# f of the SwiGLU blocks turned by VectorE and DRAM instead of by TensorE, for 10 of 11 groups

## The chip, the cores and the metric

One core of one Trainium2 chip runs the whole program. The metric is the device time of one execution in microseconds (us), and less is better. Before the change the median of three runs is 1397.9 us (1396.51 to 1398.93).

## What is computed

The program is a chain of transformer blocks over 256 tokens of width 1024: SwiGLU, gMLP, SwiGLU, SwiGLU, latent attention, SwiGLU, then a block of retention and forgetting attention, and a last SwiGLU. The change touches the five SwiGLU blocks alone. What they compute, cut to what matters:

```
def swiglu(n, w_gate, w_up, w_down):            # n: 256 x 1024
    return (silu(n @ w_gate) * (n @ w_up)) @ w_down
# w_gate, w_up: 1024 x 2816     w_down: 2816 x 1024     all float32
```

The product silu(...) * (...) is called f in the kernel: 256 tokens by 2816 columns.

## The kernel before, in words

**Tiles.** The 256 tokens are two streams of 128, t = 0 and t = 1, each an object `st` with a Python generator (`stream`). Weights come from DRAM in chunks of 128 x 1024 float32 (512 KB). `fetch` (L153) loads a chunk into `raw` (RAW = 3 buffers) from SyncE's queue (L158), and `split` (L336) makes of it a pair: `hi`, the float32r cast, by ScalarE (L337), and `lo`, the rest `raw - hi`, by VectorE (L338). The pairs have RING = 9 buffers each. `mm3` (L166) multiplies two such pairs in three matmuls (L167, L168, L169).

**Steps.** The main loop (L1134) runs over steps s. Each step fetches chunk s + 2 (AHEAD = 2), then lets stream 0 use chunk s and stream 1 use chunk s - 5 (LAG = 5). A chunk is 6 matmuls of 512 columns for each stream, so a step is 12. `later(st, n, fn)` (L192) has `fn` issued after n further chunks of that stream.

**A SwiGLU block** (`ffn`, L357) has NG = 11 groups j of 256 columns of f. `up(j)` takes four chunks (tile `g`, 512 columns: 256 of gate, 256 of up), then makes `th` by a tanh on ScalarE (L364) and f by two operations on VectorE (L365, L367). f has the tokens on the partitions. `turn(j)` (L372), two chunks later, turns it: two 128 x 128 transposes on TensorE against the identity (L376) into the PSUM tile `tr`, and `split` from there into `fth` and `ftl`, which have f's columns on the partitions. `down(j)` (L383) multiplies them with two chunks of w_down and adds to the accumulators `a`. The order is up(0), up(1), down(0), up(2), down(1), and so on: a group of six steps for every j. So f of j = 0 is used five steps after the one that ends it, f of a later j seven steps after. In the last block down(8), down(9) and down(10) stand together at the end.

There are 5 blocks x 2 streams x 11 groups = 110 turns.

**Order.** The framework's scheduler orders each engine's instructions when the program is built, by priority (the order of the program, raised inside `urgent()`) among those whose inputs it takes to be there. Each queue then runs in that order, and an instruction that waits holds those behind it. SyncE's queue carries all the loads: the chunks, and now and then gains and constants (`prepare`, L261, L265 and L266, which wait for a one-column copy on GpSimd, `touch`, L196).

**Tags.** Tiles of one tag share buffers: `th` and `f` have two each, `fth` and `ftl` three (six in the last groups of the last block).

Of the kernel before, what the change touches and what calls it, by code (L numbers as in the profile page):

```python
# [9 lines left out]
F32 = mybir.dt.float32  # L10
F32R = mybir.dt.float32r
# [5 lines left out]
P = 128  # L17
D = 1024
KD = D // P
FF = 2816  # L20
NG = FF // 256
# [88 lines left out]
def body(ctx: ExitStack, tc: tile.TileContext, a: dict, out: bass.AP, stop=None, dbg=None):  # L110
    nc = tc.nc
    V, S, G, PE = nc.vector, nc.scalar, nc.gpsimd, nc.tensor

    base = ctx.enter_context(tc.tile_pool(name="base", bufs=1))
    ring = ctx.enter_context(tc.tile_pool(name="ring", bufs=1))
    psg = ctx.enter_context(tc.tile_pool(name="psg", bufs=2, space=bass.MemoryType.PSUM))
    psa = ctx.enter_context(tc.tile_pool(name="psa", bufs=1, space=bass.MemoryType.PSUM))
    pst = ctx.enter_context(tc.tile_pool(name="pst", bufs=2, space=bass.MemoryType.PSUM))

    def f32(x):  # L120
        return x.bitcast(F32)
# [70 lines left out]
    def later(st, n, fn, *args):  # L192

        st.later.append([n + 1, fn, args])
# [128 lines left out]
    def acc_tile(st):  # L323
        return [psa.tile([P, 512], F32, name=f"a{st.t}{q}") for q in range(2)]

    def g_tile():
        return psg.tile([P, 512], F32, name="g")
# [8 lines left out]
    def split(hi, lo, src):  # L336
        S.copy(hi, src)  # L337
        V.tensor_tensor(lo, src, f32(hi), op=ALU.subtract)  # L338

    def rows_gemm(acc, lhs, w, k, first, last):  # L340

        for q in range(2):
            mm3(acc[q], sl(lhs, slice(None), k), sl(w, slice(None), slice(512 * q, 512 * q + 512)), first, last)

    def unit(st, ps, lhs=None, nq=4, nk=2, n=512):

        for q in range(nq):
            w = yield
            k_gemm(ps, lhs or st.xt, w, nk * q, q == 0, q == nq - 1, nk, n)
# [7 lines left out]
    def ffn(st, inner={}, last=False):  # L357
        fts = {}

        def up(j):  # L360
            ps = g_tile()
            yield from unit(st, ps)
            th = base.tile([P, 256], F32, name="th", tag="th", bufs=2)
            S.activation(th, ps[:, :256], AF.Tanh, scale=st.ch)  # L364
            V.scalar_tensor_tensor(th, th, 1.0, ps[:, :256], op0=ALU.add, op1=ALU.mult)  # L365
            f = base.tile([P, 256], F32, name="f", tag="f", bufs=2)
            V.scalar_tensor_tensor(f, th, st.cc, ps[:, 256:], op0=ALU.mult, op1=ALU.mult)  # L367
            fts[j] = f
            st.mark = f[:, 0:1]
            later(st, 2, turn, j)  # L370

        def turn(j):  # L372
            f = fts[j]
            tr = pst.tile([P, 4, P], F32, name="tr")
            for k in range(2):
                PE.transpose(tr[:, k, :], f[:, k * P:(k + 1) * P], ident)  # L376
            pool, n = (enter("last"), 6) if last and j > 5 else (base, 3)
            hi = pool.tile([P, 2, P], F32R, name="fth", tag="fth", bufs=n)
            lo = pool.tile([P, 2, P], F32R, name="ftl", tag="ftl", bufs=n)
            split(hi, lo, tr[:, :2, :])  # L380
            fts[j] = hi, lo

        def down(j):  # L383
            if j == 0:
                st.acc = acc_tile(st)
            for k in range(2):
                w = yield
                f = fts[j]
                rows_gemm(st.acc, f, w, k, j + k == 0, j == NG - 1 and k == 1)

        for j in range(NG):
            yield from up(j)
            if 0 < j < NG - 2 * last:
                yield from down(j - 1)
            if callable(inner.get(j)):
                inner[j]()
            elif j in inner:
                yield from inner[j]
        for j in range(NG - 1 - 2 * last, NG):
            yield from down(j)  # L400
# [614 lines left out]
    def enter(name):  # L1015
        if name not in pools:
            pools[name] = [tc.alloc_tile_pool(name=name, bufs=1), 0]
        return pools[name][0]
# [92 lines left out]
    n = len(chunks)  # L1111
# [38 lines left out]
def layout(i):  # L1150

    c = np.ascontiguousarray
    o = {}

    def cols(w, unit, nk=2):

        k, n = w.shape
        return c(w.reshape(k // (P * nk), nk, P, n // unit, unit).transpose(3, 0, 2, 1, 4)).reshape(-1, P, nk * unit)

    def rowsw(w):  # L1160

        return w.reshape(-1, P, w.shape[1])

    def gu(g, u):
        both = np.stack([g.reshape(D, NG, 256), u.reshape(D, NG, 256)], 2).reshape(D, NG * 512)
        return cols(both, 512)

    fl = [(i["ffn_w_gate"][l, k], i["ffn_w_up"][l, k], i["ffn_w_down"][l, k]) for l in range(2) for k in range(2)]
    fl.append((i["w_gate_2"][0], i["w_up_2"][0], i["w_down_2"][0]))
    for n, (g, u, d) in enumerate(fl):  # L1170
        o[f"gu{n}"] = gu(g, u)
        o[f"dn{n}"] = rowsw(d)
    o["win"] = cols(i["gmlp_w_in"][0], 512)
    o["wgo"] = rowsw(i["gmlp_w_out"][0])
    o["wdq"] = cols(i["mla_w_dq"][0], 512)
    o["wdkv"] = cols(i["w_dkv"], 320)
    uq = i["mla_w_uq"][0].reshape(512, NH, 192)
    o["wuqr"] = cols(c(uq[:, :, P:]).reshape(512, 512), 512)
    o["wuq"] = cols(c(uq[:, [0, 2, 4, 6, 1, 3, 5, 7], :P]).reshape(512, 1024), 512)
    ukv = i["w_ukv"].reshape(256, NH, 256)  # L1180
    o["wukv"] = np.concatenate([cols(c(ukv[:, :, k * P:(k + 1) * P]).reshape(256, 1024), 512) for k in range(2)])
    wo = i["mla_w_o"][0].reshape(NH, P, D)
    o["wo"] = c(wo[[0, 2, 4, 6, 1, 3, 5, 7]])
    w2 = i["w_in_2"][0]
    big = np.concatenate([w2[:, 1536:2048], w2[:, 2048:2560], w2[:, 2560:3072], w2[:, 0:512], w2[:, 512:1024],
                          w2[:, 1024:1536], w2[:, 3080:4104], w2[:, 4104:5128]], 1)
    o["w2"] = cols(big, 512)
    o["w2f"] = c(w2[:, 3072:3080].reshape(8, P, 8).transpose(1, 0, 2)).reshape(P, 64)
    o["wro"] = rowsw(i["w_ret_o_2"][0])
    o["wfo"] = rowsw(i["w_fox_o_2"][0])  # L1190
    o["wout"] = rowsw(i["w_out_2"][0])
    gl = [i["ffn_pre_g"][0, 0], i["ffn_pre_g"][0, 1], i["ffn_pre_g"][1, 0], i["ffn_pre_g"][1, 1], i["mix_pre_g"][0],
          i["mix_pre_g"][1], i["kv_norm_g"], i["kv_a_norm_g"], i["mla_q_norm_g"][0], i["g_mix_2"][0], i["g_ffn_2"][0], i["g_ret_norm_2"][0],
          np.concatenate([i["g_fox_q_2"][0]] * 2), np.concatenate([i["g_fox_k_2"][0]] * 2)]
    o["pre"] = np.stack([gl[k] for k in (4, 1, 2, 5, 3, 9)])
    o["kva"], o["qn"] = i["kv_a_norm_g"].reshape(1, 256), i["mla_q_norm_g"].reshape(1, 512)
    o["gains"] = c(np.concatenate([g.reshape(-1, P).T for g in gl], 1))
    o["ffn_post_g"] = c(i["ffn_post_g"].reshape(4, D))
    o["mix_post_g"] = c(i["mix_post_g"])
    o["gmlp_ln_g"] = c(i["gmlp_ln_g"])  # L1200
    o["gmlp_ln_b"] = c(i["gmlp_ln_b"])
    o["b_forget_2"] = c(i["b_forget_2"])
    o["ws"] = c(i["gmlp_w_s"][0].transpose(2, 0, 1)).reshape(P, 16 * P)
    o["bs"] = c(i["gmlp_b_s"][0].T)
    o["x"] = c(i["x"][0])
    o["positions"] = c(i["positions"].reshape(2, P).T)
    o["c1"], o["c2"] = constants()
    return o
# [49 lines left out]
```

## Time and profile before

| | before |
|---|---|
| median of three runs | 1397.9 us |
| profiled execution, its own time | 1396.79 us |
| its span in the profile | 1394.9 us |
| TensorE busy | 1376.0 us |
| VectorE busy | 957.0 us |
| ScalarE busy | 717.2 us |
| TensorE clock granted, mean | 1.0 of full speed |
| share of the 16 DMA engines, chunk queue | 57.7% |

The span is 1.9 us shorter than the profiled execution's time; that much lies around it. Busy times of engines overlap, so they don't add up to the span. Matmuls are pipelined: a matmul's own duration in the profile is longer than the distance to the next one's start, and that distance is what the engine's time is made of.

### The profile page before, as it was taken

How to read it: one execution, taken by the hardware profiler on the slowest of the kernel's cores; microseconds unless marked ns; L12 is line 12 of the kernel's file. 1: busy time of each engine (PE TensorE's matmuls, PEld its weight loads, DVE VectorE, ACT ScalarE, POOL GpSimd, SP SyncE). 2: the span in 40 equal slices, each digit the busy share in tenths (PEclk: the TensorE clock that was granted, in tenths of full speed). 3: DMA queues.
4: the chain of work that ended last, by engine and by line, in shares of the span. 5: the costliest groups of instructions: out<-in, count | busy, mean ns of one | idle time of the engine just before them, and what ended most of it. 6: DMA issues, size and time to landing. Idle time of an engine off the chain costs nothing.

```text
span 1394.9 us, 17750 instructions
## 1 busy us (share of the span) xinstructions
PE 1376.0 (99%) x6402; PEld 1125.1 (81%) x6402; DVE 957.0 (69%) x1530; ACT 717.2 (51%) x1043; POOL 59.7 (4%) x81
## 2 busy tenths in 40 slices
PE   8999999999999999999999999999999999999998
PEld 5888887887788887888877888888878788888887
DVE  7775579977757558775569676665677865765554
ACT  6644456555544445544456655444567544544442
POOL 0000020000000001000001010000020000000000
PEclk9999999999999999999999999999999999999999
DMA  7666667554566664666655336666544355565662
GB/s 250 201 220 185 188 250 222 157 191 151 181 191 217 186 192 143 201 220 195 188 190 179 124 130 183 202 201 191 199 137 150 119 168 183 171 190 185 192 185 88
DMA packets 71656, 254.45 MB, mean 182 GB/s; under 512 B 8592, under 2 KB 10000, under 8 KB 71184
## 3 DMA queue, kind: packets, MB, share of 16 engines
q1 hardware_dynamic: 70992, 252.78, 57.7%
q8 instruction: 51, 0.84, 0.2%
q10 hardware_dynamic: 576, 0.52, 0.1%
q14 instruction: 37, 0.30, 0.1%
HBM read 252.23 MB, written 1.05 MB: 182 GB/s over the span
## 4 chain that ended last, share of the span: by engine, by line
PE 87%; DVE 6%; ACT 2%; DMA 2%; issue 1%; POOL 1%; SPq 0%; DVEq 0%; ACTq 0%; POOLq 0%
PE g L167 16%; PE g L168 16%; PE g L169 16%; PE a L169 11%; PE a L167 11%; PE a L168 11%; DVE lo L338 2%; PE tr L376 2%; PE tr L217 2%; DMA raw<-in_win 1%; POOL sm L145 1%; ACT hi L337 1%; DMA raw<-in_gu 1%; PE tr L459 0%; PE tr L722 0%
## 5 line engine op out<-in xcount | busy, mean ns | idle before, releaser
L338 DVE TENSOR_TENSOR lo<-raw,hi 128x1024 fp32r<-128x1024 f32 (+2 forms) x462 | 560.8, 1216 | 307.2 <-ACT hi L337 305.6
L337 ACT CAST hi<-raw 128x1024 fp32r<-128x1024 f32 (+2 forms) x462 | 481.2, 1044 | 428.8 <-PE g L169 205.7
L167 PE MATMUL g<-hi,xth 128*128 128x512 f32 x1040 | 414.3, 398 | 2.2 <-ACT hi L337 1.8
L168 PE MATMUL g<-lo,xth 128*128 128x512 f32 x1040 | 407.6, 392 | 2.0 <-DVE lo L338 2.0
L169 PE MATMUL g<-hi,xtl 128*128 128x512 f32 x1040 | 406.3, 391 | 0.0
L167 PEld LDWEIGHTS g<-hi,xth 128*128 128x128 f32 x1040 | 195.4, 188 | 43.0 <-ACT hi L337 3.5
L169 PEld LDWEIGHTS g<-hi,xtl 128*128 128x128 f32 x1040 | 195.4, 188 | 41.3 <-DVE sm L255 0.2
L168 PEld LDWEIGHTS g<-lo,xth 128*128 128x128 f32 x1040 | 195.6, 188 | 41.0 <-DVE lo L338 3.7
L167 PE MATMUL a<-hi,fth 128*128 128x512 f32 x440 | 175.7, 400 | 0.0
L168 PE MATMUL a<-lo,fth 128*128 128x512 f32 x440 | 172.0, 391 | 0.0
L169 PE MATMUL a<-hi,ftl 128*128 128x512 f32 x440 | 171.9, 391 | 0.0
L169 PEld LDWEIGHTS a<-hi,ftl 128*128 128x128 f32 x440 | 82.6, 188 | 17.4
L364 ACT ACTIVATE th<-g,ch 128x256 f32<-128x256 f32 x110 | 52.3, 475 | 86.4 <-PE g L169 85.2
L168 PEld LDWEIGHTS a<-lo,fth 128*128 128x128 f32 x440 | 82.8, 188 | 15.5
L167 PEld LDWEIGHTS a<-hi,fth 128*128 128x128 f32 x440 | 82.6, 188 | 15.5
L167 PE MATMUL a<-hi,xth 128*128 128x512 f32 x232 | 94.0, 406 | 0.7 <-ACT xth L337 0.6
L168 PE MATMUL a<-lo,xth 128*128 128x512 f32 x232 | 91.0, 394 | 0.0
L169 PE MATMUL a<-hi,xtl 128*128 128x512 f32 x232 | 90.9, 395 | 0.0
L365 DVE SCALAR_TENSOR_TENSOR th<-th,g 128x256 f32<-128x256 f32 x110 | 45.9, 418 | 43.5 <-ACT th L364 43.4
L337 ACT CAST fth<-tr 128x256 fp32r<-128x256 f32 x110 | 40.5, 369 | 37.6 <-PE tr L376 37.6
L367 DVE SCALAR_TENSOR_TENSOR f<-th,cc,g 128x256 f32<-128x256 f32 x110 | 52.8, 480 | 3.5
L167 PEld LDWEIGHTS a<-hi,xth 128*128 128x128 f32 x232 | 43.6, 188 | 10.3 <-ACT xth L337 2.1
(318 smaller groups left out, 1187.0 us busy)
## 6 DMA issues: line engine op xcount, KB each, us to landing
raw<-in_gu SPq DMA_DIRECT2D x220, 512.0 KB, 3.6
raw<-in_dn SPq DMA_DIRECT2D x110, 512.0 KB, 3.9
raw<-in_w SPq DMA_DIRECT2D x40, 512.0 KB, 3.3
raw<-in_win SPq DMA_DIRECT2D x32, 512.0 KB, 4.3
raw<-in_wgo SPq DMA_DIRECT2D x16, 512.0 KB, 3.6
raw<-in_wo SPq DMA_DIRECT2D x8, 512.0 KB, 3.3
raw<-in_wout SPq DMA_DIRECT2D x8, 512.0 KB, 3.3
gn<-in_pre SPq DMA_DIRECT2D x6, 512.0 KB, 5.3
```

Of the source, the lines that this page charges most:

```text
L145: G.tensor_tensor(o, i, hp if up else hn[:, :n], op=ALU.pow)
L167: PE.matmul(o, l[0], r[0], start=start, stop=False)
L168: PE.matmul(o, l[0], r[1], start=False, stop=False)
L169: PE.matmul(o, l[1], r[0], start=False, stop=stop_)
L217: PE.transpose(tr[:, k, :], src[:, (4 * ngroup + k) * P:(4 * ngroup + k + 1) * P], ident)
L337: S.copy(hi, src)
L338: V.tensor_tensor(lo, src, f32(hi), op=ALU.subtract)
L364: S.activation(th, ps[:, :256], AF.Tanh, scale=st.ch)
L365: V.scalar_tensor_tensor(th, th, 1.0, ps[:, :256], op0=ALU.add, op1=ALU.mult)
L367: V.scalar_tensor_tensor(f, th, st.cc, ps[:, 256:], op0=ALU.mult, op1=ALU.mult)
L376: PE.transpose(tr[:, k, :], f[:, k * P:(k + 1) * P], ident)
```

## The change

f is no longer turned on TensorE, but for the last group (j = 10) of each block. For j = 0 to 9, `up` has VectorE turn f in 32 x 32 blocks, each in its place, into `ft`. One chunk later `away` writes `ft` (128 KB, rows of 1 KB) to a DRAM tile `far`; one chunk after that `back` reads it in four DMAs of 32 partitions each (32 KB, pieces of 256 bytes), which put the grid of blocks in its turned order, into `fr`; one chunk after that `parts` splits `fr` into `fth` and `ftl`. All five DMAs are on SyncE's queue. In `fr` the 256 columns of f lie on partitions and halves in another order than before, so the rows of w_down are put in that order on the host, where the weights are laid out. `ft` shares the buffers of `th`, `fr` those of `f`.

```
+    dram = ctx.enter_context(tc.tile_pool(name="dram", bufs=1, space=bass.MemoryType.DRAM))
...
             fts[j] = f
             st.mark = f[:, 0:1]
-            later(st, 2, turn, j)
+            if j == NG - 1:
+                later(st, 2, turn, j)
+                return
+
+            ft = base.tile([P, 256], F32, name="ft", tag="th", bufs=2)
+            V.transpose(ft, f)
+            later(st, 1, away, j, ft)
+
+        def away(j, ft):
+            far = dram.tile([4, 32, 4, 64], F32, name="far", bufs=4)
+            nc.sync.dma_start(far.rearrange("a i c r -> (a i) (c r)"), ft)
+            later(st, 0, back, j, far)
+
+        def back(j, far):
+            fr = base.tile([P, 4, 64], F32, name="fr", tag="f", bufs=2)
+            for c in range(4):
+                nc.sync.dma_start(fr[32 * c:32 * c + 32], far[:, :, c, :].rearrange("a i r -> i a r"))
+            later(st, 0, parts, j, fr.rearrange("p a (k i) -> p k a i", k=2))
+
+        def f_tiles(j):
+            pool, n = (enter("last"), 6) if last and j > 5 else (base, 3)
+            return tuple(pool.tile([P, 2, P], F32R, name=x, tag=x, bufs=n) for x in ("fth", "ftl"))
+
+        def parts(j, fr):
+            f = fts[j] = f_tiles(j)
+            split(*(x.rearrange("p k (a i) -> p k a i", a=4) for x in f), fr)
...
         def turn(j):
             f = fts[j]
...
-            pool, n = (enter("last"), 6) if last and j > 5 else (base, 3)
-            hi = pool.tile([P, 2, P], F32R, name="fth", tag="fth", bufs=n)
-            lo = pool.tile([P, 2, P], F32R, name="ftl", tag="ftl", bufs=n)
-            split(hi, lo, tr[:, :2, :])
-            fts[j] = hi, lo
+            fts[j] = f_tiles(j)
+            split(*fts[j], tr[:, :2, :])
...
-        o[f"dn{n}"] = rowsw(d)
+
+        d = d.reshape(NG, 4, 2, 32, D)
+        o[f"dn{n}"] = np.concatenate([d[:-1].transpose(0, 2, 1, 3, 4).reshape(-1, P, D), d[-1].reshape(2, P, D)])
```

## Rows read from the trace of the kernel before

**Rows 1.** Page, part 1: busy time and share of the span of each engine.

```profile
PE 1376.0 (99%) x6402; PEld 1125.1 (81%) x6402; DVE 957.0 (69%) x1530; ACT 717.2 (51%) x1043; POOL 59.7 (4%) x81
```

**Rows 2.** Page, part 4: the chain that ended last, by engine, by line.

```profile
PE 87%; DVE 6%; ACT 2%; DMA 2%; issue 1%; POOL 1%; SPq 0%; DVEq 0%; ACTq 0%; POOLq 0%
PE g L167 16%; PE g L168 16%; PE g L169 16%; PE a L169 11%; PE a L167 11%; PE a L168 11%; DVE lo L338 2%; PE tr L376 2%; PE tr L217 2%; DMA raw<-in_win 1%; POOL sm L145 1%; ACT hi L337 1%; DMA raw<-in_gu 1%; PE tr L459 0%; PE tr L722 0%
```

**Rows 3.** Waits of PE, the longest in total: us, times, longest.

```profile
PE tr L217 <- DVE x L299: 3.7, 5, 1.7
```

**Rows 4.** The chain, stretch 100 to 190 us (first SwiGLU block), by line.

```profile
by line: PE g L167 21.4%; PE g L168 21.3%; PE g L169 21.2%; PE a L167 11.2%; PE a L169 11.2%; PE a L168 11.1%; PE tr L376 2.7%
```

**Rows 5.** Timeline of SyncE's queue, one group: start us, us, issues of chunks.

```profile
121.51 8.87 SPq L158 DMA_DIRECT2D raw<-in_gu  x4
132.46 3.06 SPq L158 DMA_DIRECT2D raw<-in_dn  x2
138.37 8.87 SPq L158 DMA_DIRECT2D raw<-in_gu  x4
```

**Rows 6.** Groups by line and form, ACT: busy us, mean ns | idle before, releaser.

```profile
L337 ACT CAST hi<-raw 128x1024 fp32r<-128x1024 f32 x454 | 476.0, 1050 | 424.6 <-PE g L169 204.7 <-PE a L169 155.3 <-DMA raw<-in_gu 28.8
...
L337 ACT CAST xth<-y 128x256 fp32r<-128x256 f32 x16 | 6.3, 402 | 7.0 <-DVE y L228 6.8
```

**Rows 7.** The same view, DVE: a chunk's rest, operations of 256 columns.

```profile
L338 DVE TENSOR_TENSOR lo<-raw,hi 128x1024 fp32r<-128x1024 f32 x454 | 554.9, 1224 | 303.0 <-ACT hi L337 301.4
L367 DVE SCALAR_TENSOR_TENSOR f<-th,cc,g 128x256 f32<-128x256 f32 x110 | 52.8, 480 | 3.5
...
L338 DVE TENSOR_TENSOR ftl<-tr,fth 128x256 fp32r<-128x256 f32 x110 | 42.4, 417 | 5.9 <-ACT fth L337 5.8
...
L338 DVE TENSOR_TENSOR xtl<-y,xth 128x256 fp32r<-128x256 f32 x16 | 6.5, 419 | 0.3
...
L273 DVE TENSOR_SCALAR pg<-pg 128x256 f32<-128x256 f32 x24 | 5.9, 288 | 7.3 <-DMA pg<-in_ffn_post_g 7.0 <-DMA pg<-in_mix_post_g 0.4
```

**Rows 8.** Tile raw: the time from issue to landing.

```profile
DMA to landing us min/median/max: 3.0/3.6/9.8
```

**Rows 9.** Timeline of PE around one turn: start us, us, engine, line, operation.

```profile
131.92 0.39 PE L167 MATMUL a<-hi,fth 128*128 128x512 f32 x1
...
132.37 0.40 PE L169 MATMUL a<-hi,ftl 128*128 128x512 f32 x1
132.61 0.38 PE L376 MATMUL tr<-cst,f 128*128 128x128 f32 x2
132.74 0.48 PE L167 MATMUL a<-hi,fth 128*128 128x512 f32 x1
...
133.29 0.39 PE L169 MATMUL a<-hi,ftl 128*128 128x512 f32 x1
```

**Rows 10.** Timeline of ACT and DVE: how one f comes about.

```profile
127.36 0.47 ACT L364 ACTIVATE th<-g,ch 128x256 f32<-128x256 f32 x1 [1.67 <-PE g L169]
...
128.32 0.48 DVE L367 SCALAR_TENSOR_TENSOR f<-th,cc,g 128x256 f32<-128x256 f32 x1
```

**Rows 11.** DMA view: queues (packets, MB, share); issues (KB each, median us to landing).

```profile
q1 hardware_dynamic: 70992, 252.78, 57.7%
...
q10 hardware_dynamic: 576, 0.52, 0.1%
...
out<-h SPq DMA_DIRECT2D x4, 128.0 KB, 1.9
...
wfr<-in_w2f SPq DMA_DIRECT2D x1, 32.0 KB, 3.9
```

**Rows 12.** Timeline of SyncE's queue where gains are loaded among the chunks.

```profile
79.52 0.33 SPq L265 DMA_DIRECT2D pg<-in_ffn_post_g  x1
79.90 0.42 SPq L266 DMA_DIRECT2D gn<-in_pre  x1
```

**Rows 13.** Stretches: us, busy us of PE, PEld, DVE, ACT, POOL, clock, DMA, GB/s.

```profile
70.00:80.00 10.00, 10.00 (x46) 8.28 (x45) 6.03 (x8) 4.40 (x6) 1.32 (x2) 1.00 0.60 191
80.00:90.00 10.00, 10.00 (x47) 8.21 (x46) 7.60 (x17) 4.39 (x6) 0.00 (x0) 1.00 0.80 265
```

## The prediction, made before the changed kernel was run

> **What bounds the kernel now.** I read the busy shares first, then the chain that ended last, then who waits for whom. TensorE is busy for 1376.0 us of the span of 1394.9 [rows 1]. The chain lies on it for 87% [rows 2], and its longest wait by total is 3.7 us [rows 3]. Inside a SwiGLU block the chain is TensorE and nothing else, and the turn of f, L376, is 2.7% of it [rows 4]. So in the stretches that the change touches, time is the sum of the distances between matmul starts, and whatever leaves TensorE there leaves the span, as long as TensorE goes on being fed.
>
> How is it fed? A group of six chunks takes 138.37 - 121.51 = 16.86 us [rows 5], so a step is 2.81 us. ScalarE's cast of a new chunk has 424.6 us of idle time before it, most of it ended by TensorE: it waits for a pair to come free [rows 6]. The ring of 9 is full, then. A pair is freed by stream 1, five steps behind, so the pair of chunk c is written three steps before stream 0 needs it: 8.4 us, less 1.05 for the cast [rows 6] and 1.22 for the rest [rows 7], leaves a **lead of 6 us**. The load before that has slack of its own: with three raw buffers it is issued 8.4 - 2.3 = 6.1 us before the cast and lands in 3.6 [rows 8], 2.5 us early.
>
> **The change, part by part.**
>
> *Removed: 100 of 110 turns on TensorE.* The two transposes and what they disturb are costed by starts, not by durations. From the matmul ahead (132.37) to the third behind (133.29) is 0.92 us. Without a turn two matmuls take 0.45 (131.92 to 132.37), so three take 0.68, and one turn costs 0.24 us [rows 9]. A second reading: 2.7% of 16.86 us for two turns is 0.23 each [rows 4]. 100 turns are **24 us**. The durations of the two transposes, 0.38 us together [rows 9], overlap their neighbours, and I don't take them.
>
> *Added on VectorE: 100 block transposes of 128 x 256.* No row shows one. Operations of 256 columns take 0.29 us (one source, SBUF) to 0.48 (f) [rows 7]; I take 0.42, as most of these rows do. That is 29 to 48 us more on an engine that is 69% busy [rows 1]. TensorE's time hides it; only its 0.42 us within f's way counts.
>
> *Moved: the split.* It reads SBUF instead of PSUM. Rows for either source exist: 0.417 against 0.419 us on VectorE [rows 7], and 0.40 us on ScalarE [rows 6]. Nothing.
>
> *Added: f's trip through DRAM.* After the last matmul of `up` f is ready at 128.80, 1.44 us after the tanh began at 127.36 [rows 10]. Then the block transpose, 0.4. The write of 128 KB: 1.9 us at the idle end of the program (out<-h), or as slow as the 3.9 of wfr, which shared the queue with chunks [rows 11]; I take 2.5. Four reads: 0.33 us of SyncE for each issue [rows 12], the last begins 1.0 us after the first; to landing 1.9 to 3.9, and I take 3.9, since wfr has just this size and neighbourhood. The split, 0.8. Likely sum: 1.4 + 0.4 + 2.5 + 1.0 + 3.9 + 0.8 = 10.0 us. Ends: 7.3 with the short DMAs and the short transpose; 13.9 with the long write and transpose, and a chunk's rest (1.2) in front of f and again in front of the split. Available are steps of now 16.86 - 0.48 = 16.4 us a group, 2.73 each: 4.5 of them, 12.3 us, for j = 0 (from the middle of the step that ends f), 6.5 of them, 17.7 us, for j > 0. So 90 trips are hidden to the last, and the 10 of j = 0 cost between 0 and 1.6 us each. I take 0.3 each: **3 us**.
>
> *Added to SyncE's queue: ten issues a group and the waits of `away` and `back`.* 3.3 us of issuing in 16.4. `away` waits for VectorE, `back` for the write's landing, and the chunk loads queue behind both, as do the gains of `prepare`. The scheduler places them when it takes them to be ready, so a hold is what the chip is later than the plan: at best nothing, at worst a whole write, 3.9 us. The cover is 2.5 us, then the lead of 6. The trace has an experiment on this: at 79.52 and 79.90 two loads of gains go between the chunks [rows 12], with DMA engines at 0.80 of their time, and TensorE stays busy for 10.00 of 10.00 us on both sides [rows 13]. A group of the changed kernel has a disturbance of about that size, and then another. I take no cost.
>
> *Added to the DMA engines.* 100 x 256 KB is 26 MB on 253 at 57.7% [rows 11]: by bytes, 6 points more. By packets: 640 small ones a turn; the 576 of q10, about 0.9 KB each, took 0.1% of 16 engines, some 0.04 us each, so 1.6 us of each engine a turn, 3.1 a group, 19 points. Between 64% and 77% there is room.
>
> *Added: shared buffers.* `ft` needs a buffer of `th` until the write has read it, `fr` one of `f` until the split, some two steps each in six, and the two streams are a step apart. GpSimd's one-column copies (`touch`) read an f a little later still, as before, and nothing is put into GpSimd's queue. I see no wait that outlasts a step: nothing.
>
> **Sum.** The profiled execution took 1396.79 us (span 1394.9, 1.9 around it), 1.1 below the median. 1396.8 - 24 + 3 = 1375.8; forecast **1376 us**. Its own range is 1371 (24 us gained, and a little at the boundaries) to 1380.
>
> **The rivals.**
>
> *The trip is late and half the gain goes back.* Where trips take 13.9 us and more, j = 0 loses 1.6 us ten times; and ScalarE and VectorE, held by a split whose data is late, pass on some of it elsewhere. That is 16 us or a little more: 1380 to 1397. For it: two DRAM latencies in a row, each guessed from one or four rows. Against: 17.7 us of cover for nine in ten.
>
> *SyncE's queue becomes the bound, and the kernel is slower.* As the program is written, `away` comes between two chunk loads and waits for an f of the step just done. If it is placed so, the next loads stand behind it: tanh to f 1.4, transpose 0.4, write 1.9 to 3.9, four issues 1.3, the chunk itself 3.6, cast and rest 2.3 make 10.9 to 12.9 us, with a chunk's rest in front up to 14.1, against 12.3 us until that chunk is used. A loss of 0 to 1.8 us a turn; at 1 us it is 100 us, 1396.8 - 24 + 100 = 1473. It decides from 0.24 us a turn, where the gain is gone. For it: the queue runs in order, and both waits are new. Against: the gains' loads above. The Trainium skill, DMA: Bandwidth & Descriptors, section Anatomy of one DMA, says that DMA engines don't wait for semaphores: the wait sits on the issuing sequencer, so everything behind it is held. It adds that a write's completion can be surprisingly late when HBM is the target. By that rule the long end would be the one to take, 1.8 us a turn: an estimate of 1553 us. The trace before has writes to DRAM only at its idle end, so it can't say.
>
> *The change saves TensorE's work and not the time.* Feeding becomes the pace: three raw buffers go round in 3.6 + 2.3 + 0.1 = 6.0 us, 2.0 a chunk; ten issues add 0.55 a chunk: 2.55 against the new step of 2.73. Were chunks to land 0.6 us later for the new traffic, that would be 2.75, and with a hold more, and the old step of 2.81 comes back: 1394 to 1402. For it: the sum is close. Against: issues fall into gaps of the queue, which spends most of its time waiting for a buffer.
>
> **How the numbers follow.** The forecast has 0.58, the late trip 0.18, SyncE's queue 0.16, the feeding pace 0.08. What measurement can tell from no change is about 0.2%, 2.8 us. Faster by more: 0.58 and 0.13 of the late trip, 0.71. Within it: 0.05 of the late trip and 0.04 of the pace, 0.09. Slower: 0.16 and 0.04, 0.20. The range of 8 in 10 takes in the forecast, the late trip and most of the pace, and leaves out SyncE's rival and a gain beyond the transposes: 1369 to 1400.
>
> **What would show it.** Right: L376 with 20 transposes, no wait of TensorE for fth or for hi in a block's middle, six chunks in 16.4 us, VectorE's transpose at 0.3 to 0.5 us. The late trip: waits of TensorE or ScalarE for `fr` or fth, mostly at j = 0. SyncE's rival: chunk loads bunched behind `back`, casts that wait for raw instead of for TensorE, TensorE waiting for hi and lo. The forecast is wrong if groups in a block's middle take over 16.9 us.

## The result: 1432.8 us, slower by 2.5%

The changed kernel takes 1432.83 us (median of four runs, 1430.2 to 1436.01) against 1397.87: a ratio of 1.0252, 95% interval 1.0228 to 1.0275. The forecast was 1376, faster. The profiled execution took 1436.01 us with a span of 1434.1.

The page, parts 1 and 4, of the changed kernel, beside [rows 1, 2]:

```profile
PE 1381.5 (96%) x6202; PEld 1107.9 (77%) x6202; DVE 993.2 (69%) x1630; ACT 714.9 (50%) x1041; POOL 56.1 (4%) x81
...
PE 63%; DMA 12%; DVE 12%; ACT 6%; issue 4%; SPq 1%; POOL 1%; DVEq 0%; ACTq 0%; POOLq 0%
```

The 200 transposes are gone (6402 instructions of TensorE to 6202), and the chain is on TensorE for 63% only. DMA, VectorE and ScalarE have taken the place: TensorE is now fed late. ScalarE and VectorE by form say who is late, beside [rows 6, 7]:

```profile
L338 ACT CAST hi<-raw 128x1024 fp32r<-128x1024 f32 x454 | 473.5, 1052 | 302.3 <-DMA raw<-in_gu 124.8 <-DMA raw<-in_dn 50.0 <-PE a L170 43.3
...
L338 ACT CAST fth<-fr 128x256 fp32r<-128x256 f32 x100 | 40.3, 405 | 70.3 <-DMA fr<-far 70.1
```

```profile
L376 DVE STREAM_TRANSPOSE ft<-f 128x256 f32<-128x256 f32 x100 | 44.4, 444 | 2.4
```

The casts of chunks waited for TensorE before, 360 us in all, that is, for a free pair of a full ring [rows 6]. Now most of their waiting is for the chunk itself (124.8 + 50.0 us). So the ring is often no longer full. A second wait is new: 70.1 us for f to come back. VectorE's transpose takes 0.444 us, as taken (0.42).

Do chunks take longer to land? Tile raw, beside [rows 8]:

```profile
DMA to landing us min/median/max: 3.0/4.2/8.4
```

The median is 0.6 us more. But e_dead_one and e_pair7 below, which beat the kernel before, have 4.2 too, so it is not this. The timeline of SyncE's queue over one group shows what it is, beside [rows 5]:

```profile
129.20 0.38 SPq L381 DMA_DIRECT2D far<-ft  x1
133.80 3.67 SPq L159 DMA_DIRECT2D raw<-in_gu  x3
139.23 0.33 SPq L381 DMA_DIRECT2D far<-ft  x1
139.61 4.77 SPq L387 DMA_DIRECT2D fr<-far  x8
144.78 0.35 SPq L159 DMA_DIRECT2D raw<-in_gu  x1
145.25 0.83 SPq L159 DMA_DIRECT2D raw<-in_dn  x2
146.18 0.38 SPq L381 DMA_DIRECT2D far<-ft  x1
150.73 4.29 SPq L159 DMA_DIRECT2D raw<-in_gu  x3
```

A group takes 146.18 - 129.20 = 17.0 us, where 16.4 were forecast. Between 137.5, when the third chunk load is out, and 144.78 no chunk load is issued: the queue stands at a write whose f is being made, then issues eight reads, some of which wait for that write. When the loads could have gone, VectorE shows: a chunk load waits for its buffer, and the buffer is free when `lo` of the chunk three before is done.

```profile
139.12 1.18 DVE L339 TENSOR_TENSOR lo<-raw,hi 128x1024 fp32r<-128x1024 f32 x1
...
140.87 1.23 DVE L339 TENSOR_TENSOR lo<-raw,hi 128x1024 fp32r<-128x1024 f32 x1 [0.56 <-ACT hi L338]
...
143.48 1.23 DVE L339 TENSOR_TENSOR lo<-raw,hi 128x1024 fp32r<-128x1024 f32 x1 [0.74 <-ACT hi L338]
```

The buffers come free at 140.30, 142.10 and 144.71, and the three loads go out at 144.78, 145.25 and 145.71: 4.5, 3.2 and 1.0 us late. The stand at the write, until 139.23, holds no load up; the reads, and the wait for the write's landing among them, do. Even the f written at 129.20 comes back only with the one written at 139.23. ScalarE's timeline shows both trips:

```profile
124.83 0.47 ACT L365 ACTIVATE th<-g,ch 128x256 f32<-128x256 f32 x1 [1.06 <-PE g L170]
...
137.27 0.47 ACT L365 ACTIVATE th<-g,ch 128x256 f32<-128x256 f32 x1 [1.42 <-PE g L170]
...
143.47 0.41 ACT L338 CAST fth<-fr 128x256 fp32r<-128x256 f32 x1
145.99 0.41 ACT L338 CAST fth<-fr 128x256 fp32r<-128x256 f32 x1 [2.12 <-DMA fr<-far]
```

From tanh to both parts the second takes 9.5 us (137.27 to 145.99, 0.41 for the cast, and 0.42 for VectorE's rest), almost the forecast 10.0. The first takes 19.5 us (124.83 to 143.47, and the same 0.83), more than its cover of 17.7, because the queue lets its reads wait behind the other stream's write.

### The profile page after: what moved, and what is told of

It reads as the page before. It is cut to its first block, busy times and chain, and to the rows that moved or that the text cites. A ratio compares the mean times of both kernels' runs of the same rounds, so it can differ in the third digit from the quotient of the medians.

```text
span 1434.1 us, 18356 instructions
## 1 busy us (share of the span) xinstructions
PE 1381.5 (96%) x6202; PEld 1107.9 (77%) x6202; DVE 993.2 (69%) x1630; ACT 714.9 (50%) x1041; POOL 56.1 (4%) x81
## 3 DMA queue, kind: packets, MB, share of 16 engines
q1 hardware_dynamic: 142992, 279.03, 60.6%
## 4 chain that ended last, share of the span: by engine, by line
PE 63%; DMA 12%; DVE 12%; ACT 6%; issue 4%; SPq 1%; POOL 1%; DVEq 0%; ACTq 0%; POOLq 0%
PE g L169 12%; PE g L170 11%; PE g L168 11%; PE a L170 8%; PE a L169 8%; PE a L168 8%; DMA raw<-in_gu 5%; DVE lo L339 5%; ACT hi L338 4%; DMA raw<-in_dn 3%; PE tr L218 1%; DMA raw<-in_w 1%; DMA raw<-in_win 1%; POOL sm L146 1%; SPq L387 1%
## 5 line engine op out<-in xcount | busy, mean ns | idle before, releaser
L168 PE MATMUL g<-hi,xth 128*128 128x512 f32 x1040 | 403.5, 396 | 6.9 <-ACT hi L338 4.8
L168 PEld LDWEIGHTS g<-hi,xth 128*128 128x128 f32 x1040 | 196.0, 188 | 54.3 <-ACT hi L338 10.1
L168 PE MATMUL a<-hi,fth 128*128 128x512 f32 x440 | 160.6, 397 | 7.0 <-ACT fth L338 5.3
L338 ACT CAST fth<-fr 128x256 fp32r<-128x256 f32 x100 | 40.3, 405 | 70.3 <-DMA fr<-far 70.1
L169 PEld LDWEIGHTS a<-lo,xth 128*128 128x128 f32 x232 | 44.1, 190 | 13.1 <-DVE lo L339 5.4
```

Source lines behind the costliest of these rows:

```text
L168: PE.matmul(o, l[0], r[0], start=start, stop=False)
L169: PE.matmul(o, l[0], r[1], start=False, stop=False)
```

## The experiments

All times are device us; the kernel before, timed again beside each of them, took 1397.2 to 1398.9. "Above" is above e_no_trip.

**What TensorE gives: e_no_trip.** The transpose on VectorE stays, the trip goes; `parts` splits `ft`, so the grid of blocks keeps its order and the product is not the one wanted:

```
-            later(st, 1, away, j, ft)
+            later(st, 3, parts, j, ft.rearrange("p (k a i) -> p k a i", k=2, a=4))
```

> VectorE's block transposes stay, the trip through DRAM is left out: parts splits ft as it is, three chunks after up, so the grid of blocks isn't turned (that part of the computation is left out). f's tag has three buffers instead of two. If the loss lies in the trip (queue, traffic or lateness): TensorE's 24 us come through, 1371 to 1378 us. If VectorE's transposes or the new order on VectorE and ScalarE cost: 1385 or more.

1373.98, ratio 0.982 (0.9805 to 0.9834): 24.9 us less. So step one holds in full, VectorE's work costs nothing, and all 59 us between this and the changed kernel come with the trip.

**The trip on another queue: e_act_trip, e_pool_trip.** All five DMAs issued by ScalarE, or by GpSimd:

```
-            nc.sync.dma_start(far..., ft)
+            nc.scalar.dma_start(far..., ft)        (e_pool_trip: nc.gpsimd)
```

> The changed kernel with away and back issued from ScalarE's queue instead of SyncE's; the same bytes and packets. Queue: SyncE's chunk loads go out as before the change, 1374 to 1390 us, with some loss to the issues on ScalarE (ten a group at about 0.4 us) and to casts held behind the wait for the write. Traffic: 1425 to 1440. Lateness: 1425 to 1440.

> The changed kernel with away and back issued from GpSimd's queue, which has little else to do; the same bytes. Queue: 1374 to 1390 us, and above that only what the small copies and powers on GpSimd lose at the ends of blocks. Traffic: 1425 to 1440. Lateness: as slow as the changed kernel or slower, if the trip takes longer from there.

1495.39 (ratio 1.0698, 1.0677 to 1.072) and 1502.81 (1.074, 1.0723 to 1.0757): both far worse, and above every range given for them; of the theories only lateness, in e_pool_trip's words, allows it. ScalarE's waits, of e_act_trip and then of e_pool_trip:

```profile
ACT fth L338 <- DMA fr<-far: 298.7, 52, 9.7
```

```profile
ACT fth L338 <- DMA fr<-far: 245.5, 86, 8.2
```

With SyncE's queue left to the chunks, the split waits up to 9.7 us for f, and the casts of chunks stand behind it on ScalarE. A trip on SyncE's queue is bad; one that is late at a split placed early is worse.

**The trip without its use: e_dead_trip, e_dead_sp, e_dead_pool, e_dead_away, e_dead_back, e_dead_stale.** The split takes `ft`, as in e_no_trip (all six leave the same part out), and the DMAs run beside it, so lateness of what they bring can't matter. The core of e_dead_sp:

```
+            later(st, 3, parts, j, ft.rearrange("p (k a i) -> p k a i", k=2, a=4))
             later(st, 1, away, j, ft)
...
-            fr = base.tile([P, 4, 64], F32, name="fr", tag="f", bufs=2)
+            fr = base.tile([P, 4, 64], F32, name="fr", tag="fr", bufs=1)
...
-            later(st, 0, parts, j, fr.rearrange("p a (k i) -> p k a i", k=2))
```

e_dead_trip was the first of them, with `fr` in th's buffers; it took 1425.12, but a new th then waited for reads, and e_dead_sp, with a buffer of its own, replaces it.

> As the kernel without the trip, but the write and the four reads are made on SyncE's queue as in the changed kernel; nobody uses what they bring (the grid of blocks isn't turned). Theory of the queue (chunk loads stand behind away and back on SyncE): still slow, 1415 to 1440 us. Theory of traffic (many small packets slow the chunks): the same, 1415 to 1440. Theory of lateness (ScalarE, VectorE and TensorE wait for fr): the wait is gone, 1372 to 1385.

> The write and the four reads on SyncE's queue as in the changed kernel, with nobody using what they bring: parts splits ft (the grid of blocks isn't turned), ft and f in the changed kernel's buffers, fr in one of its own, so that no other tile waits for the trip. Queue and traffic: 1415 to 1430 us. Lateness alone: 1372 to 1380.

e_dead_pool has the five DMAs on GpSimd's queue, e_dead_away the write alone, e_dead_back the four reads alone, from the input x, so that they wait for no write:

> The same unused trip from GpSimd's queue; the same bytes, and no chunk load and no split stands behind it (the grid of blocks isn't turned). Traffic: as slow as the unused trip on SyncE's queue, 1415 to 1430 us. Queue or lateness: 1372 to 1385.

> Of the unused trip on SyncE's queue the write alone, without the reads (the grid of blocks isn't turned). If what holds the queue is away's wait for VectorE: 1400 us or more. If it is the reads, by their issues or their wait for the write: 1373 to 1385.

> Of the unused trip on SyncE's queue the four reads alone, of pieces of 256 bytes of the input x, which wait for no write (the grid of blocks isn't turned). If the reads' issues hold the queue: 1395 us or more. If it is the wait for the write's landing: 1373 to 1385.

In e_dead_stale the reads take the tile that the group before wrote, so no write in flight is waited for:

```
-            later(st, 0, back, j, far)
+            later(st, 0, back, j, fars.pop(st.t, far))
+            fars[st.t] = far
```

> The unused trip on SyncE's queue, but each read takes what the same stream wrote a group earlier, so it waits for no write that is still on its way (the grid of blocks isn't turned, and the data is a group old; it isn't used). If the loss of the whole trip, over that of write and reads each by itself, is back's wait for the write with the chunk loads behind it: 1380 to 1395 us. If it is that ten DMAs a group crowd the queue and the DMA engines: 1412 to 1425.

| unused trip | us | ratio (95%) | above |
|---|---|---|---|
| e_dead_away | 1376.57 | 0.9836 (0.982, 0.9852) | 2.6 |
| e_dead_pool | 1384.09 | 0.9892 (0.9877, 0.9907) | 10.1 |
| e_dead_back | 1384.98 | 0.9899 (0.9885, 0.9914) | 11.0 |
| e_dead_stale | 1414.53 | 1.0125 (1.0102, 1.0148) | 40.6 |
| e_dead_sp | 1422.03 | 1.0175 (1.0147, 1.0204) | 48.1 |

The same bytes cost 10 us from GpSimd's queue and 48 from SyncE's, so at least 38 of them are the queue and not the DMA engines. In e_dead_pool chunks still take 4.3 us to land in the median, as in e_dead_sp (4.2). What remains to the changed kernel, 1432.8 - 1422.0 = 11 us, comes with the use of `fr`; I read it as f's lateness at the split, by this difference alone. The writes alone and the eight reads alone cost 14 together, the two in one queue 48: the price is not a sum, and eight reads by themselves are not the cause. And the wait for the write's landing, my first suspect, is only 7.5 of it (e_dead_stale); e_dead_back's range for that theory was met, and the theory was wrong all the same.

**Splitting later: e_sp_pin, e_mix_pin, e_pool_pin.** Groups 1 to 9 alone, the split some chunks later and held there on ScalarE and VectorE; the reads on SyncE's queue three chunks later and held there too (e_sp_pin), on GpSimd's (e_mix_pin), or all DMAs on GpSimd's (e_pool_pin):

```
-            if j == NG - 1:
+            if j in (0, NG - 1):
...
-            later(st, 0, parts, ...)
+            later(st, 3, parts, ...)               (e_sp_pin: back by 3 in its place)
...
-            split(*(x.rearrange("p k (a i) -> p k a i", a=4) for x in f), fr)
+            tc.keep_in_program_order(S.copy(hi, fr))
+            tc.keep_in_program_order(V.tensor_tensor(lo, fr, f32(hi), op=ALU.subtract))
```

> A complete kernel: the changed one with the reads three chunks later, kept behind the chunk loads written ahead of them on SyncE's queue, and the split kept behind what is written ahead of it on ScalarE and VectorE; groups 1 to 9 go by DRAM, 0 and 10 by TensorE; one buffer more for f's tag. If the two costs are the wait for the write on SyncE and the split that is placed before its data: 1380 to 1395 us, faster than the kernel before the change. If crowding: 1410 or more.

> A complete kernel: the write on SyncE's queue, the reads and their wait on GpSimd's, the split three chunks later and kept behind what is written ahead of it; groups 1 to 9. Wait and placing: 1376 to 1390 us, since no chunk load stands behind a wait and SyncE issues one DMA a turn. Crowding of the DMA engines: 1395 or more.

> A complete kernel: write and reads on GpSimd's queue as in the run of 1503 us, but the split three chunks later and kept behind what is written ahead of it; groups 1 to 9. If those 1503 us came from a split that is placed before its data: 1378 to 1392 us. If from traffic or from GpSimd's own holds: over 1400.

1423.74 (1.0189, 1.0161 to 1.0216), 1404.44 (1.005, 1.0034 to 1.0065) and 1404.92 (1.0045, 1.0031 to 1.0058). On GpSimd's queue a late split takes back 98 of e_pool_trip's loss; on SyncE's it brings 9. So off SyncE's queue it is lateness, and on it the queue. None beats the kernel before, and all three missed the ranges below 1396 that I had given them. e_mix_pin and e_pool_pin are still 28 to 29 us above e_no_pin below, the same kernel without a trip, and the unused trip from GpSimd costs 10. In e_mix_pin TensorE waits 10.7 us for `fth`; where the rest comes from is open.

**Which part of the queue's load: e_dead_late, e_dead_one.** From e_dead_sp (1422.0), the first moves the write three chunks away from its f, the second takes away six of eight reads a group:

```
-            later(st, 1, away, j, ft)
+            later(st, 4, away, j, ft)
```

> The unused trip on SyncE's queue, as in e_dead_sp (1422.03), but the write is issued four chunks after f instead of one, so that f and its block transpose are long done when the write's turn comes. All ten issues a group stay on the queue, and the reads still follow their write one chunk later. The two parts are split from ft, so the grid of blocks is not turned. Theory 'the write's wait for f' (ready chunk loads stand behind a write whose f is still being made): the wait is gone, 1383 to 1397, and chunk loads are no longer held before far. Rival 'eight read issues' (eight issues of 0.33 to 0.43 us in the midst of a group's chunk loads): 1410 to 1425, little change.

```
-            for c in range(4):
-                nc.sync.dma_start(fr[32 * c:32 * c + 32], far[:, :, c, :].rearrange("a i r -> i a r"))
+            nc.sync.dma_start(fr.rearrange("p a r -> p (a r)"), far.rearrange("a i c r -> (a i) (c r)"))
```

> The unused trip on SyncE's queue, as in e_dead_sp (1422.03), but f comes back in one read of 128 KB in place of four of 32 KB, so a group has four issues of the trip instead of ten. The write keeps its place behind f and its wait. The two parts are split from ft, so the grid of blocks is not turned. Rival 'eight read issues': 1383 to 1395. Theory 'the write's wait for f': 1408 to 1422, since the wait stays where it was. If the loss needs both, a wait and reads that push it into the chunk loads' way: 1395 to 1408, and then e_dead_late lies there too.

e_dead_late 1420.52 (1.0163, 1.0148 to 1.0178), e_dead_one 1376.13 (0.9854, 0.9837 to 0.987). Moving the write is worth 1.5 us, within the intervals, and beside the two writes the number of reads decides, more cleanly than its own theory had it: 2.1 us above e_no_trip, under its range. SyncE's queue in e_dead_sp, then in e_dead_one, a group each:

```profile
133.89 0.43 SPq L382 DMA_DIRECT2D far<-ft  x1
135.27 0.33 SPq L159 DMA_DIRECT2D raw<-in_gu  x1
138.40 1.75 SPq L388 DMA_DIRECT2D fr<-far  x4
141.78 0.34 SPq L382 DMA_DIRECT2D far<-ft  x1
142.22 1.05 SPq L159 DMA_DIRECT2D raw<-in_gu  x2
143.54 1.75 SPq L388 DMA_DIRECT2D fr<-far  x4
...
150.99 0.43 SPq L382 DMA_DIRECT2D far<-ft  x1
```

```profile
129.50 0.42 SPq L382 DMA_DIRECT2D far<-ft  x1
131.49 0.33 SPq L159 DMA_DIRECT2D raw<-in_dn  x1
131.87 0.42 SPq L382 DMA_DIRECT2D far<-ft  x1
133.46 0.33 SPq L387 DMA_DIRECT2D fr<-far  x1
134.21 0.33 SPq L159 DMA_DIRECT2D raw<-in_dn  x1
136.67 0.32 SPq L387 DMA_DIRECT2D fr<-far  x1
137.09 8.69 SPq L159 DMA_DIRECT2D raw<-in_gu  x4
145.82 0.42 SPq L382 DMA_DIRECT2D far<-ft  x1
```

In e_dead_sp reads and writes cut the chunk loads apart: between 135.27 and 142.22 no chunk load goes out, while four reads and a write are waited for and issued; the group takes 17.1 us. In e_dead_one the four loads of gate and up stand together, and the trip's DMAs are issued in the gaps in which a chunk load would have to wait for a buffer anyway: 16.32 us, the pace without a trip.

The traces let one add this up. For each of 457 chunk loads I take the time from the end of the `lo` that frees its buffer to the load's issue, and what SyncE did in between (worked out from the traces; us in the whole run, 14 to 23 of it the few hundredths of a us that every load takes):

| | loads late, in all | issuing reads | standing at a read | standing at a write |
|---|---|---|---|---|
| before | 19 | | | |
| e_no_trip | 20 | | | |
| e_dead_pool | 21 | | | |
| e_dead_away | 27 | | | 2 |
| e_dead_back | 64 | 30 | 4 | |
| e_dead_one | 84 | 16 | 36 | 3 |
| e_dead_late | 190 | 94 | 39 | 3 |
| e_dead_stale | 329 | 117 | 21 | 100 |
| changed kernel | 375 | 200 | 57 | 38 |
| e_dead_sp | 382 | 144 | 53 | 104 |

With the trip on GpSimd's queue chunk loads go out as without one. In the changed kernel the eight reads and what they wait for make 257 of 375 us. In e_dead_late hardly a load stands behind a write any more, and the kernel is as slow, so the write's wait for f is not what the price hangs on. The sums are not losses: e_dead_late has half the sum of e_dead_sp and nearly its time, and the 84 us of e_dead_one cost 2.

One thing the two runs can't part: with fewer reads the framework also laid out the queue in another order, so what a read costs by its 0.44 us of issue and what by where it pushes the others is open: e_dead_back's eight reads, in an order of their own, hold loads for 30 us and not 144. (The reads of e_dead_one also have rows of 1 KB for pieces of 256 bytes; e_dead_pool limits what the pieces can cost to 10 us.)

**The same cure in a whole kernel: e_late_pin, e_no_pin, e_pair, e_pair7.** e_late_pin writes three chunks after f and reads a chunk later (groups 1 to 9, held split); e_no_pin is e_no_trip with groups 1 to 9 and the held split:

> A whole and used trip for groups 1 to 9 (90 turns off TensorE, 21.6 us): the write on SyncE's queue three chunks after f, the reads a chunk later, the split two chunks after them and held in the order of the program on ScalarE and VectorE. If the write's wait for f is most of what SyncE's queue costs, 1397.9 - 21.6 + some 13 for the write and the reads by themselves = 1389, 1383 to 1397, which would beat both kernels. If the reads' issues or a late split cost as much in any place: 1403 to 1425.

> As e_no_trip (1373.98; no trip, the two parts split from ft, the grid of blocks not turned), but for groups 1 to 9 only and with the split held in the order of the program, as in e_mix_pin (1404.44). If holding the split in place costs nothing by itself: 1373.98 + 2.4 for the ten turns that come back, 1374 to 1380, and e_mix_pin's 28 us more are the trip's traffic and lateness. If the held order costs it: 1388 to 1405.

e_no_pin: 1376.18 (0.9846, 0.9832 to 0.9861); holding the split is free. e_late_pin: 1441.69 (1.0318, 1.0302 to 1.0333), a plain miss. Its SyncE queue waits most at the write, and the wait is put down to the rest of a split, which the write doesn't read:

```profile
SPq L381 <- DVE ftl L398: 153.9, 66, 4.9
```

The timeline has another answer:

```profile
135.67 0.45 DVE L376 STREAM_TRANSPOSE ft<-f 128x256 f32<-128x256 f32 x1
136.04 0.38 DVE L398 TENSOR_TENSOR ftl<-fr,fth 128x256 fp32r<-128x256 f32 x1
136.15 3.32 SPq L381 DMA_DIRECT2D far<-ft  x2
```

The write goes out 0.03 us after the end of a transpose (135.67 + 0.45), before that rest is done, and counted in order 84 of the 90 writes go within 0.1 us of the end of their own f's transpose. So the write stands three chunks later in the program, and in the queue it still comes where its f has just been made; the run doesn't show what a late write costs. That moving the write does not mend the queue rests on e_dead_late, where 42 of 100 writes still go that close. So I cut the reads instead. e_pair writes f of stream 1's group j and of stream 0's group j + 1, which are ready a step apart, side by side into one tile, and four reads of 64 KB bring both (groups 1 to 9, held split; f is made in th's buffers, of which there are three):

```
+            far = dram.tile([4, 32, 4, 2, 64], ...)     (one for both, h = 1 for stream 1)
+            nc.sync.dma_start(far[:, :, :, h, :].rearrange("a i c r -> (a i) c r"), ft...)
+            if not h:
+                later(st, 1, back, j, far)
...
+                nc.sync.dma_start(fr[32 * c:32 * c + 32].rearrange("i a h r -> i a (h r)"),
+                                  far[:, :, c].rearrange("a i h r -> i a (h r)"))
```

> A whole and used trip for groups 1 to 9 with half the read issues: f of stream 1's group j and of stream 0's group j + 1, which are ready a step apart, are written into one DRAM tile side by side and come back in four reads of 64 KB (pieces of 512 bytes) for both, two chunks after the later write; so a group has six issues of the trip in place of ten. The split comes two chunks after the reads, held in the order of the program. 90 turns leave TensorE, 21.6 us. If the number of read issues among the chunk loads is the price (e_dead_one 1376.1 against e_dead_sp 1422.0): 1397.9 - 21.6 + 3 to 15 for writes, four reads and traffic, 1379 to 1392, faster than both kernels. If four reads in a row hold the queue as eight do, or the writes in 256-byte pieces cost more than whole rows: 1400 to 1425.

1396.72 (0.9995, 0.9985 to 1.0004): 27 us better than e_sp_pin, but no faster than before, 5 us over its range. In the first block's middle its groups take 16.32 us (writes at 132.24, 148.56, 164.88); at the end of one it is different, as SyncE's queue shows for e_no_pin and for e_pair:

```profile
164.28 8.49 SPq L159 DMA_DIRECT2D raw<-in_dn  x4
175.20 0.33 SPq L159 DMA_DIRECT2D raw<-in_win  x1
...
178.70 0.39 SPq L159 DMA_DIRECT2D raw<-in_win  x1
...
180.60 27.60 SPq L159 DMA_DIRECT2D raw<-in_win  x9
```

```profile
166.82 0.33 SPq L159 DMA_DIRECT2D raw<-in_dn  x1
...
177.70 0.33 SPq L159 DMA_DIRECT2D raw<-in_win  x1
...
181.58 0.53 SPq L389 DMA_DIRECT2D far<-ft  x1
182.21 0.75 SPq L159 DMA_DIRECT2D raw<-in_win  x1
...
187.81 1.75 SPq L401 DMA_DIRECT2D fr<-far  x4
...
190.08 20.07 SPq L159 DMA_DIRECT2D raw<-in_win  x7
```

e_pair is 2.5 us behind in the block's middle already (166.82 against 164.28), and no more at the first chunk of the next block (177.70 against 175.20). The second is 3.5 us later, the third 9.5 (190.08 against 180.60): the last write of stream 1 and its reads stand in front of that block's loads. So e_pair7 takes the trip only for stream 0's groups 2 to 8 and stream 1's 1 to 7:

```
-            if j in (0, NG - 1):
+            if not 2 - st.t <= j <= 8 - st.t:
```

> e_pair (1396.7) with the trip in the middle of a block alone: stream 0 takes it for groups 2 to 8 and stream 1 for groups 1 to 7, always as a pair in four reads; the other 40 turns stay on TensorE (where the streams share a group's order of w_down, f is written in the turned order of columns first, as two VectorE operations). 70 turns leave TensorE: 16.8 us. By issue times of the chunks, e_pair loses nothing against the kernel without a trip in the middle of a block, and 2 to 4 us at each end of one, where the last trips and the unpaired ones stand. If that reading holds: 1397.8 - 16.8 + 2 to 8 for the traffic and what is left at the starts, 1383 to 1389, faster than both kernels. If the loss is not bound to the ends but goes with the number of trips: 1397.8 - 16.8 + 16 = 1397, no change.

**1388.57** (ratio 0.9945, 0.9929 to 0.9961), in its range: 8.7 us faster than the kernel before and 44 faster than the change. Of the 16.8 us of its 70 turns about half comes through. Its chunk loads are 105 us late in all, where e_pair's are 152. At the block's end it loses nothing more against e_no_pin (first three chunks of the next block at 181.78, 185.32 and 187.22, each 6.6 us later); the 6 us by which it is behind there come from the first block's first groups. Its page, part 1:

```profile
PE 1362.1 (98%) x6262; PEld 1112.3 (80%) x6262; DVE 980.4 (71%) x1610; ACT 717.5 (52%) x1043; POOL 58.7 (4%) x81
```

## Why the prediction was wrong, point by point

- **100 turns, 24 us.** Right: e_no_trip gives 24.9. Counting by starts, and not by the transposes' durations, was the right way to read [rows 9].
- **VectorE's transposes, the split from SBUF.** Right: 0.444 us each against 0.42, hidden; the cast 0.405 us.
- **f's trip, 10.0 us and 3 us of cost.** Half right. The trip that stands behind no other takes 9.5 us. But I priced it as if each f had the queue to itself: of the two in the group shown, one takes 19.5, outside my ends of 7.3 to 13.9, and the use of `fr` costs about 11 us (by difference), not 3.
- **SyncE's queue, "I take no cost".** This step failed: it is 38 us (e_dead_sp against e_dead_pool). I had divided the ten issues, 3.3 us, over a group of 16.4 and seen room, when what counted was one stretch in which they stood in a row in front of loads: 4.5, 3.2 and 1.0 us late in the group shown, 375 in the run. The gains' loads [rows 12, 13] were the wrong analogy. They are two issues, and they held up one load, by 1.0 us (78.22 + 1.23 against 80.42):

```profile
78.22 1.23 DVE L338 TENSOR_TENSOR lo<-raw,hi 128x1024 fp32r<-128x1024 f32 x1
...
80.42 0.38 SPq L158 DMA_DIRECT2D raw<-in_gu  x1
```

  e_dead_away and e_dead_back show that writes alone and reads alone pass for 3 to 11 us; two writes and eight reads among the chunk loads don't.
- **The DMA engines.** Their share is 60.6%, under both of my figures (64 and 77), of a longer span; that there is room agrees with e_dead_pool, whose 10 us are the most that traffic can cost.
- **The rival "SyncE's queue becomes the bound".** It had the place and the signs right (loads bunched behind `back`, casts waiting for raw), a chance of only 0.16, and too high a price: 100 us of loss forecast, 59 measured. It put the loss down to waits for f and the write; by e_dead_late and e_dead_stale neither wait is the cause by itself. The rule of the Trainium skill, DMA: Bandwidth & Descriptors, section Anatomy of one DMA, that a wait sits on the issuing sequencer, agrees with the timeline: no chunk load passes a waiting write. Its other half, that a write's completion to HBM can be surprisingly late, and the 1553 us estimated with it, are not borne out here: writes land in 2.9 us in the median and 6.5 at most, and that wait is worth 7.5 us of the whole.
- **The late trip, the feeding pace.** The first is real, 11 us on top, by difference. For the second, chunks do land the 0.6 us later that I named as its condition, but e_dead_one has the same 4.2 us and the full pace: landing time by itself is not the bound.
- **The groups.** "Wrong if groups in a block's middle take over 16.9 us": 17.0.

The 59 us over e_no_trip are then, by differences between runs: at most 10 of traffic, 38 or more of SyncE's queue, 11 of late splits. That the queue costs the 38 is shown; how issue times, waits and the order in the queue share them is not.

## What to carry to other kernels

In this kernel the queue that feeds the bounding engine had no spare time that could be read off as a share: its price for added DMAs went with how many stood in a row in front of a load whose buffer was free, and with what those waited for. So count DMA issues, not bytes, join small transfers where the layout allows it (here two streams' reads), and keep them away from the places where the load order changes. Before that, find in the trace when each load's buffer comes free, and compare it with the load's issue. And where an in-order engine uses a transfer's result, put that use later than the transfer's worst place in the queue, not its own latency: that brought back 98 us on GpSimd's queue here.

## What the runs showed of the hardware that was not expected

TensorE's clock, 1.0 of full speed throughout before, dropped for moments in the changed kernel. Stretches around a block's end (us, busy us of PE, PEld, DVE, ACT, POOL, clock, DMA share, GB/s):

```profile
190.00:195.00 5.00, 3.50 (x16) 2.21 (x14) 2.07 (x4) 2.56 (x5) 2.78 (x3) 1.00 0.30 116
195.00:199.00 4.00, 3.47 (x9) 2.77 (x9) 3.08 (x4) 1.42 (x2) 0.00 (x0) 0.57 0.59 197
199.00:205.00 6.00, 3.35 (x15) 2.44 (x13) 2.24 (x4) 2.20 (x5) 0.55 (x1) 1.00 0.99 415
```

After 5 us in which TensorE was busy for 3.50, the clock granted falls to 0.57 in the mean of 4 us, near the lower of its two levels (1.2 GHz, 0.5), and then returns. Over the whole run the mean is 0.993; 1434.1 x 0.007 is some 10 us of TensorE's time at the most, a part of the losses above and not an addition to them. e_no_trip and e_pair7, which keep TensorE fed, stand at 1.0, the four executions of e_dead_sp at 0.989 to 0.994. So a late feed was followed here by a second loss, a stretch at the lower clock; but not every slow feed is, since e_late_pin, with 1441.7 us, stands at 0.999.
